# Layer 0 of a two-layer transformer block: feeding it from a transposed x, in eight granules of shift and scale

## The chip, the core and the metric

The kernel runs on one core of a Trainium2 chip. A core has a matrix engine (PE, TensorE), VectorE (DVE), ScalarE (ACT), GpSimd (POOL) and SyncE (SP), which here only issues DMAs. Each engine takes its instructions in program order; they meet through semaphores. DMAs issued from SP, ACT or POOL run on 16 DMA engines that the core's queues share. On-chip memory has 128 partitions; PE writes to eight PSUM banks of 128 x 512 float32. The metric is device time of the whole launch in microseconds.

## What is computed

The input x has 256 tokens of 2048 features; a second input c conditions both layers. Layer 0 mixes with differential attention, layer 1 with a state-space scan (SSD), and each layer ends in a SwiGLU feed-forward part. All in float32.

```python
c_act = silu(c)
for i in range(2):
    ada = c_act @ ada_w[i] + ada_b[i]                  # 2048 x 12288
    shift1, scale1, gate1, shift2, scale2, gate2 = split(ada, 6)
    h = rms_norm(x, norm1_g[i]) * (1 + scale1) + shift1
    m = diff_attention(h, ...) if i == 0 else mamba2_ssd(h, ...)
    x = x + gate1 * m
    h = rms_norm(x, norm2_g[i]) * (1 + scale2) + shift2
    x = x + gate2 * ((silu(h @ w_gate) * (h @ w_up)) @ w_down)
```

`diff_attention` projects h with `da_w_in` (2048 x 6144) to q, k and v of 16 heads; q and k are normalized per 64 features and rotated (a quarter of the features), two softmaxes per head are subtracted, and the result is normalized and projected with `da_w_out`.

## The kernel before

Nearly all time goes into streaming weights. A *unit* is 256 rows by 512 columns of a weight matrix, 512 KB, laid out on the host so that one DMA brings it into a `raw` buffer (7 of them, `rawp`). `split_unit` (line 244) issues the DMA on SP, lets ACT round it to a high part `wh` and, one unit later through the list `lagging`, lets DVE form the low part `wl = raw - wh`; there are four buffers of each. h is split in the same way into `ah` and `al`. `products` (276) then multiplies a unit with one block of 128 tokens in six matmuls of 512 columns (high x high, high x low, low x high for two groups of 128 features), so a unit costs twelve for both blocks.

The order of instructions is written out by a small planner while the program is built. `fifo` holds what is still to be written: weight units (`u`, at most four), units used raw (`a`, at most four) and plain calls (`c`). `push_unit` (260) and `push_raw` (267) write the DMA and casts at once and queue the matmuls; `pop` (224) writes the oldest. Each written weight unit is a `tick` (193): it lets one step of every generator in `active` be written (epilogues and attention heads are generators that yield between dependent steps), starts a new attention part from `pending` every four steps (`PACE`), and may write *jobs*. A job is one unit of 128 rows by 1024 columns of `ada_w` for one of the later shift, scale and gate vectors: a DMA and one DVE multiply-add into `acc` (`ada_job`, 426). `room` (185) holds jobs back when the charges booked for DVE or DMA are more than `METER` = 10,000 ns ahead of those for PE. A finished gate half is summed over the partitions by two POOL all-reduces (`fin_gate`, 508); a finished shift or scale half is summed by PE into columns (`to_cols`, 460).

**The start of layer 0.** The conditioning c comes in as 16 rows and is transposed by PE with an identity that POOL makes first; so are three tables of columns (norm gains and biases, class `Columns`, 361). `push_mods` (763) computes shift1 and scale1 for a quarter, 512 features, each from eight raw units: for each group of 128 rows PE multiplies c, repeated 32 times, with the unit in one of four 32-column strips; then ACT copies the bank, and `finish` sums and turns it into columns with four small matmuls. x is loaded as two blocks of tokens between the first units; ACT squares and scales it, PE transposes each quarter (32 transposes of 128 x 128 in all), and `Norm.finish` (546) applies scale and shift on DVE and splits h. `item` (1071) sets what happens before each raw unit: from the second quarter on it interleaves, per quarter, eight weight units of the first four (`N_EARLY`) projections, with the sixteen raw units of the next. `push_early` (1004) adds each such projection up over the quarters: two units share two PSUM banks, then ACT copies (first quarter) or DVE adds the banks to `part`.

After the last quarter the four early projections are completed (`complete`, 855: for q and k the generator `epilogue`, 807, with POOL's reciprocal root of the norms and rotary products `rt`), and the other eight of the twelve projections run over all 2048 rows in eight units each. `complete` of a q or k of head group 2 or 3 must first let all three parts of attention of the group two before have begun; if they haven't, it writes steps until they have. Attention (`attend`, 892) uses POOL for the norm of a head group's output (`oss`, `orr`). The output projection follows; before its last group's units `flush_steps` (216) writes all steps that are left. Jobs run in the order shift2, scale2, gate1; what is left of them is written by `flush_jobs` in the output projection.

`cols0.st` and the tiles for c and for the normalized x are taken from buffers that attention uses later (`raw`, pool `dp`).

Of the kernel before, what the change touches and what calls it, by code (L numbers as in the profile page):

```python
# [33 lines left out]
N_EARLY = 4  # L34
EPI = 3
ADA_UNITS = 140
# [51 lines left out]
def block_kernel(ctx: ExitStack, tc: tile.TileContext, x, c, positions, norm1_g, norm2_g, ada_w, ada_b,  # L88
                 ffn_gu, ffn_dn, da_in, da_out, q_g, k_g, lq1, lk1, lq2, lk2, subln_g,
                 ssd_in, conv_w, conv_b, dt_bias, a_log, d_skip, ssd_ng, ssd_out, out, upto="all"):  # L90
    nc = tc.nc
    ada_quarters = Units(ada_w, D, 256, chunks_of(2 * D))
    ada_rows, o = [], ada_quarters.end
# [173 lines left out]
    def push_raw(w, row, col, fn):  # L267
# [93 lines left out]
    class Columns:  # L361


        def __init__(self, groups):

            self.groups = groups
            self.st = rawp.tile([128, 8, 128], F32, tag="raw", name="stage")
            for i, (_, aps) in enumerate(groups):
                r = 0
                for a in aps:  # L370
                    pool.dma_start(self.st[r:r + a.shape[0], i, :], a)
                    r += a.shape[0]

        def finish(self, i):
            t = self.groups[i][0]
            n = t.shape[1]
            ps = bank("wk")
            pe.transpose(ps[:, :n], self.st[:n, i, :], ident[:n, :n])
            dve.tensor_copy(t, ps[:, :n])

    gcols = const.tile([128, 65], F32, name="gcols")
    bias_cols = [const.tile([128, 64], F32, name=f"bias{l}") for l in range(2)]
    bias_rows = ada_b.rearrange("l (v k p) -> l v k p", v=6, p=128)
    crows = rowp.tile([16, 128], F32, tag="acc", name="crows", bufs=2)
    sp.dma_start(crows, c.rearrange("o (k p) -> (o k) p", p=128))
    cols0 = Columns([
                     (gcols, [norm1_g.rearrange("l (k p) -> (l k) p", p=128),
                              norm2_g.rearrange("l (k p) -> (l k) p", p=128), subln_g]),
                     (bias_cols[0], [bias_rows[0, v:v + 2].rearrange("v k p -> (v k) p") for v in (0, 3)]),
                     (bias_cols[1], [bias_rows[1, v:v + 2].rearrange("v k p -> (v k) p") for v in (0, 3)])])  # L390
    ps = bank("wk")
    pe.transpose(ps[:, :16], crows, ident[:16, :16])
    cT = const.tile([128, 16], F32, name="cT")
    act.activation(cT, ps[:, :16], AF.Silu)
# [276 lines left out]
    pha = ExitStack()  # L671
    dp = pha.enter_context(tc.tile_pool(name="dp", bufs=1))
    cT32 = dp.tile([128, 512], F32, tag="on", name="cT32", bufs=1).rearrange("p (k m) -> p k m", m=32)
# [11 lines left out]
    lv = cols0.st[:, 4:6, :].rearrange("p a (i d) -> p (a i) d", d=64)  # L685
# [77 lines left out]
    def push_mods(q, item):  # L763

        sl = slice(4 * q, 4 * q + 4)
        for vec in range(2):
            st = {}

            def use(raw, u, st=st, vec=vec):
                if u == 0:  # L770
                    st["ps"] = bank(("po", "wk")[vec])
                for a in range(2):
                    k = 2 * u + a
                    g = k % 4
                    pe.matmul(st["ps"][32 * g:32 * g + 32, :], cT32[:, k, :], raw[:, a, :], start=(k < 4),
                              stop=(k >= 12), tile_position=(0, 32 * g), skip_group_check=True)
                if u == 7:
                    st["sb"] = tmp("adasb")
                    act.copy(st["sb"], st["ps"])

            def finish(st=st, vec=vec):
                ps2 = bank("wk")
                for i in range(4):
                    pe.matmul(ps2[:, i:i + 1], st["sb"][:, i * 128:(i + 1) * 128], c32, start=True, stop=True)
                t = S0 if vec else T0
                dve.tensor_tensor(t[:, sl], ps2[:, :4], b_cols[0, vec][:, sl], op=ALU.add)
                if vec:
                    dve.scalar_tensor_tensor(t[:, sl], t[:, sl], 1.0, n1c[0][:, sl], op0=ALU.add, op1=ALU.mult)
            for u in range(8):
                item(8 * vec + u)  # L790
                push_raw(ada_quarters, u * 256, vec * D + q * 512, lambda raw, u=u, use=use: use(raw, u))
                if u == 2 and vec == 1:
                    call(shift_finish)
                if u == 5 and vec == 1:
                    call(lambda: [norm_a.transposes(b, q, xns[b, q]) for b in range(2)])
            if vec == 0:
                shift_finish = finish
        return finish

# [7 lines left out]
    def epilogue(nm, dst, n, src):  # L807
# [22 lines left out]
        for b in range(2):  # L830
            rt = dp.tile([128, 8, 16], F32, tag="rt", name="rt", bufs=2)
# [23 lines left out]
    def complete(n, src, in_psum):  # L855
# [6 lines left out]
        if in_psum:  # L862
            while ahead():
                step_all()
            if i < 2:
                tiles = []
                for b in range(2):
                    t = dp.tile([128, 512], F32, tag="qn", name="qn", bufs=2)
                    act.copy(t, src[b])
                    tiles.append(t)  # L870
                src = tiles

        def steps(src=src):
            while ahead():
                yield
            if i == 2:
                v = dp.tile([128, 2, 512], F32, tag="v", name="v", bufs=2)
# [3 lines left out]
            else:  # L881
                dst = dp.tile([128, 4, 256], F32, tag=f"{nm}T", name=f"{nm}T", bufs=2)
# [9 lines left out]
    def attend(hg, qb, heads):  # L892
# [22 lines left out]
        for cc in range(2):  # L915
            m, n = mx[:, 4 * cc:4 * cc + nh], sums[:, 4 * cc:4 * cc + nh]
            dve.tensor_reduce(m, s3[cc], axis=AX.X, op=ALU.max, negate=True)
            ex = dp.tile([128, 512], F32, tag=f"e{cc}", name=f"e{cc}", bufs=(3, 1)[cc])
# [52 lines left out]
        on = dp.tile([128, 512], F32, tag="on", name="on", bufs=1)  # L971
# [32 lines left out]
    def push_early(n, q, half):  # L1004
        hg, i = keys[n]
        if half == 0:
            part[n, "bk"] = Banks()
        bk = part[n, "bk"]

        def run(u):  # L1010
            for b in range(2):
                products(bk()[b], norm_a.h[q][b], half, u, 512, half == 0, half == 1)
        push_unit(wi, q * 512 + half * 256, i * D + hg * 512, 512, run)
        if half == 1:
            def collect():
                if q == 0:
                    tg = ("oh", "ol")[n % 2]
                    part[n] = [op_.tile([128, 4, 128], F32, tag=tg, name=f"part{tg}")
                               .rearrange("p a n -> p (a n)") for b in range(2)]
                for b in range(2):  # L1020
# [50 lines left out]
    def item(i, q):  # L1071
# [8 lines left out]
        if p == 3:  # L1080
            flush()
# [598 lines left out]
```

## Time and profile before

| | us |
|---|---|
| median of 3 runs | 2696.89 (2692.03 to 2699.83) |
| the profiled execution | 2695.24 |
| its span (first to last instruction) | 2692.9 |
| PE busy | 2644.4 (98%) |
| DVE, ACT, POOL busy | 1912.2, 1346.4, 253.8 |
| HBM read | 678.43 MB |

A line of an instruction listing gives start, duration, engine, line of the program, operation, output and inputs by tile name, shape and count; in brackets stands how long the engine was idle before it, and what ended that. Matmul durations overlap: two matmuls of 512 columns start 0.23 us apart while each shows 0.39. `PEclk` is the clock that PE was granted (1.00 is full). A line of a group gives the count, the busy time and the mean of one in ns. Line 115 is the helper through which all PE and DVE instructions pass; they are told apart by their tiles.

### The profile page before, as it was taken

How to read it: one execution, taken by the hardware profiler on the slowest of the kernel's cores; microseconds unless marked ns; L12 is line 12 of the kernel's file. 1: busy time of each engine (PE TensorE's matmuls, PEld its weight loads, DVE VectorE, ACT ScalarE, POOL GpSimd, SP SyncE). 2: the span in 40 equal slices, each digit the busy share in tenths (PEclk: the TensorE clock that was granted, in tenths of full speed). 3: DMA queues.
4: the chain of work that ended last, by engine and by line, in shares of the span. 5: the costliest groups of instructions: out<-in, count | busy, mean ns of one | idle time of the engine just before them, and what ended most of it. 6: DMA issues, size and time to landing. Idle time of an engine off the chain costs nothing.

```text
span 2692.9 us, 35740 instructions
## 1 busy us (share of the span) xinstructions
PE 2644.4 (98%) x13205; PEld 2188.2 (81%) x13205; DVE 1912.2 (71%) x2154; ACT 1346.4 (50%) x1996; POOL 253.8 (9%) x242
## 2 busy tenths in 40 slices
PE   6999998999999999999999999999999999999999
PEld 2577886888888888888999989988888888888887
DVE  2579897888888886777777787786654444446776
ACT  3356774554444444445646556665554444444443
POOL 1032331102111110001000010000000000000001
PEclk8999999999999999999999999999999999999999
DMA  8989997788999997785567576666746555556885
GB/s 316 323 279 313 332 313 270 246 298 319 341 352 332 333 334 248 276 289 201 165 218 241 198 250 215 224 219 199 224 153 190 188 191 190 189 188 230 282 289 182
DMA packets 192558, 682.98 MB, mean 254 GB/s; under 512 B 22128, under 2 KB 30624, under 8 KB 191104
## 3 DMA queue, kind: packets, MB, share of 16 engines
q1 hardware_dynamic: 190256, 678.59, 72.9%
q0 software_dynamic: 1696, 2.03, 0.3%
q8 instruction: 103, 1.69, 0.2%
q14 instruction: 71, 0.58, 0.1%
q10 hardware_dynamic: 432, 0.10, 0.0%
HBM read 678.43 MB, written 2.20 MB: 253 GB/s over the span
## 4 chain that ended last, share of the span: by engine, by line
PE 92%; DVE 3%; DMA 2%; ACT 1%; issue 1%; POOL 0%; SPq 0%; ACTq 0%; DVEq 0%
PE mm L115 73%; PE wk L115 15%; PE po L115 4%; DMA raw<-in_da_w_in 1%; DMA raw<-in_ada_w 1%; DVE wl L115 1%; DVE acc L115 1%; ACT wh L250 0%; DVE hm L115 0%; DVE res L115 0%; DVE x L115 0%; DVE partol L115 0%; ACT hm L560 0%; DMA raw<-in_da_w_out 0%; ACT ah L566 0%
## 5 line engine op out<-in xcount | busy, mean ns | idle before, releaser
L250 ACT CAST wh<-raw 128x1024 fp32r<-128x1024 f32 (+1 forms) x888 | 925.8, 1046 | 1143.5 <-PE mm L115 756.8
L115 DVE TENSOR_TENSOR wl<-raw,wh 128x1024 fp32r<-128x1024 f32 (+1 forms) x888 | 1117.8, 1266 | 533.4 <-ACT wh L250 532.1
L115 PE MATMUL mm<-wh,ah 128*128 128x512 f32 (+1 forms) x2560 | 1016.5, 397 | 5.7 <-ACT ah L566 2.9
L115 PE MATMUL mm<-wl,ah 128*128 128x512 f32 (+1 forms) x2560 | 999.8, 391 | 0.6 <-DVE wl L115 0.6
L115 PE MATMUL mm<-wh,al 128*128 128x512 f32 (+1 forms) x2560 | 999.6, 390 | 0.0
L115 PEld LDWEIGHTS mm<-wh,ah 128*128 128x128 f32 x2560 | 482.3, 188 | 125.2 <-issue 16.7
L115 PEld LDWEIGHTS mm<-wh,al 128*128 128x128 f32 x2560 | 482.2, 188 | 102.9 <-DVE al L115 1.5
L115 PEld LDWEIGHTS mm<-wl,ah 128*128 128x128 f32 x2560 | 482.6, 189 | 97.9 <-DVE wl L115 2.0
L115 DVE SCALAR_TENSOR_TENSOR acc<-raw,cT,acc 128x1024 f32<-128x1024 f32 x300 | 386.0, 1287 | 0.5
L514 POOL PARTITION_ALL_REDUCE gate<-acc x16 | 54.7, 3460 | 969.7 <-DVE acc L115 954.8
L115 PE MATMUL wk<-wl,ah 128*128 128x512 f32 x360 | 140.2, 389 | 0.0
L115 PE MATMUL wk<-wh,ah 128*128 128x512 f32 x360 | 140.2, 389 | 0.0
L115 PE MATMUL wk<-wh,al 128*128 128x512 f32 x360 | 140.1, 389 | 0.0
L115 PE MATMUL mm<-ah,wh 128*128 128x256 f32 x720 | 118.8, 284 | 0.0
L115 PE MATMUL mm<-al,wh 128*128 128x256 f32 x720 | 117.7, 283 | 0.0
L115 PE MATMUL mm<-ah,wl 128*128 128x256 f32 x720 | 117.7, 283 | 0.0
L115 PEld LDWEIGHTS mm<-ah,wh 128*128 128x128 f32 x720 | 100.2, 192 | 0.1
L115 PEld LDWEIGHTS mm<-ah,wl 128*128 128x128 f32 x720 | 100.2, 192 | 0.0
L115 PEld LDWEIGHTS mm<-al,wh 128*128 128x128 f32 x720 | 100.2, 192 | 0.0
L466 POOL PARTITION_ALL_REDUCE row<-acc x16 | 54.9, 3478 | 382.7 <-DVE acc L115 382.7
L115 PEld LDWEIGHTS wk<-wl,ah 128*128 128x128 f32 x360 | 67.6, 188 | 14.4 <-DVE wl L115 0.4
L115 PEld LDWEIGHTS wk<-wh,ah 128*128 128x128 f32 x360 | 67.6, 188 | 14.2
(307 smaller groups left out, 2020.6 us busy)
## 6 DMA issues: line engine op xcount, KB each, us to landing
raw<-in_ada_w SPq DMA_DIRECT2D x384, 512.0 KB, 5.0
raw<-in_ffn_w_gate_up SPq DMA_DIRECT2D x352, 512.0 KB, 4.3
raw<-in_ffn_w_down SPq DMA_DIRECT2D x176, 512.0 KB, 4.8
raw<-in_ssd_w_in SPq DMA_DIRECT2D x136, 512.0 KB, 4.5
raw<-in_da_w_in SPq DMA_DIRECT2D x96, 512.0 KB, 5.3
raw<-in_ssd_w_out SPq DMA_DIRECT2D x64, 512.0 KB, 4.4
raw<-in_da_w_out SPq DMA_DIRECT2D x32, 512.0 KB, 5.3
raw<-in_ssd_w_in SPq DMA_DIRECT2D x24, 384.0 KB, 4.9
```

What stands on the lines that cost most here:

```text
L115: return fn(dst, *a, **k)
L250: act.copy(wh[:, :, :n], raw[:, :, :n])
L466: pool.partition_all_reduce(row[:, o], acc[:, o], 128, ReduceOp.add)
L514: pool.partition_all_reduce(mods["G", key][:, o:o + 512], acc[:, i * 512:(i + 1) * 512], 128, ReduceOp.add)
```

## The change

Five things change.

- **Tables.** The host lays c, the norm gains and the biases of layer 0's and 1's shifts and scales out as one array of 128 x 209, brought in by one DMA on SP; the SSD columns are three DMAs on ACT's queue. `Columns` and its six transposes go.
- **x.** The host adds a transposed copy `x_t` of x, four pieces of 512 KB with features on the partitions; they are loaded first. `token_sums` squares them on ACT and adds on DVE, PE sums over the partitions, POOL forms the reciprocal root, and `scale_tokens` has PE spread it over all partitions and DVE multiply the transposed x with it. No transposes of x remain. x itself is loaded into the same tiles later, while the eighth projection is queued.
- **Granules.** Shift and scale come in eight granules of 256 features; the host interleaves 256 columns of each in one unit of 512 columns, so that a granule is eight raw units, one bank and one `finish`. The raw units have a ring of nine buffers of their own (`A_BUFS`) in a pool `first`, which is closed before pool `dp` opens. `norm_pair` applies scale and shift on ACT for two groups of 128 features and splits h.
- **Partial sums.** Six projections instead of four are added up early, over eight granules instead of four quarters: each unit has two banks of its own, and its two blocks are copied (first granule) or added by DVE. The six units of a granule are interleaved with the eight raw units of the next.
- **Jobs.** Gate1 comes before shift2 and scale2; jobs may start from the fifth granule on instead of from the second quarter.

```diff
-N_EARLY = 4
+N_EARLY = 6
+A_BUFS = 9
...
-        raw = rawp.tile([128, 2, 512], F32, tag="raw", name="raw")
+        raw = ring.tile([128, 2, 512], F32, tag="araw", name="araw", bufs=A_BUFS)
...
+    cols = const.tile([128, 209], F32, name="cols")
+    sp.dma_start(cols, columns_in)
...
-    def push_mods(q, item):
...
+    def push_mods(g, item):
+        st = {}
+        sl = slice(2 * g, 2 * g + 2)
+        def use(raw, u):
+            if u == 0:
+                st["ps"] = bank(("po", "wk")[g % 2])
...
+        def finish():
+            ps2 = bank("wk")
+            for i in range(4):
+                pe.matmul(ps2[:, i:i + 1], st["sb"][:, i * 128:(i + 1) * 128], c32, start=True, stop=True)
+            dve.tensor_tensor(T0[:, sl], ps2[:, 0:2], b_cols[0, 0][:, sl], op=ALU.add)
+            dve.tensor_tensor(S0[:, sl], ps2[:, 2:4], b_cols[0, 1][:, sl], op=ALU.add)
+            dve.scalar_tensor_tensor(S0[:, sl], S0[:, sl], 1.0, n1c[0][:, sl], op0=ALU.add, op1=ALU.mult)
+        for u in range(8):
+            item(u)
+            push_raw(ada_first, u * 256, g * 512, lambda raw, u=u: use(raw, u), first)
...
+    def token_sums():
+        held["sums"] = [tmp("xsum") for _ in range(2)]
+        for q in range(4):
+            sq = rawp.tile([128, 2, 512], F32, tag="raw", name="xsq").rearrange("p a n -> p (a n)")
+            act.activation(sq, x_quarter(q), AF.Square)
+            dve.tensor_reduce(held["sums"][q // 2][:, (q % 2) * 256:(q % 2 + 1) * 256],
+                              sq.rearrange("p (k t) -> p t k", k=4), axis=AX.X, op=ALU.add)
...
+    def scale_tokens():
+        ps = bank("wk")
+        for b in range(2):
+            o = slice(b * 128, b * 128 + 128)
+            pe.matmul(ps[:, o], held["r"][:, o], ident, start=True, stop=True)
+        for q in range(4):
+            v = x_quarter(q).rearrange("p (k t) -> p k t", k=4)
+            dve.tensor_tensor(v, v, ps[:, None, 0:256].to_broadcast([128, 4, 256]), op=ALU.mult)
+    def norm_pair(g):
...
+        hm = tmp("hm").rearrange("p (k t) -> p k t", k=2)
+        for i in range(2):
+            k = 2 * g + i
+            act.activation(hm[:, i, :], x_feature(k), AF.Identity, bias=T0[:, k:k + 1], scale=S0[:, k:k + 1])
+        act.copy(h[:, o, :], hm)
+        dve.tensor_tensor(l[:, o, :], hm, h[:, o, :].bitcast(F32), op=ALU.subtract)
...
-    def push_early(n, q, half):
...
+    def push_early(n, g):
...
+                products(bk()[b], norm_a.h[q][b], half, u, 512, True, True)
+        push_unit(wi, g * 256, i * D + hg * 512, 512, run)
+        def collect():
...
+                if g == 0:
+                    act.copy(part[n][b], bk()[b])
+                else:
+                    dve.tensor_tensor(part[n][b], part[n][b], bk()[b], op=ALU.add)
...
+    ada_job(0, 2, fin_gate("m0"), gate=True)
     ada_job(0, 3, fin_shift("f0", b_cols[0, 3]))
     ada_job(0, 4, fin_scale("f0", b_cols[0, 4], n2c[0]))
-    ada_job(0, 2, fin_gate("m0"), gate=True)
...
+    for q in range(4):
+        sp.dma_start(x_quarter(q), x_t[q])
...
+    def item(i, g):
+        if g == 0:
+            if i in (2, 4):
+                call(token_rstd if i == 2 else scale_tokens)
             return
+        at["p"] += 1
+        if i == 1:
+            call(finishes[g - 1])
+        elif i == 2:
+            call(lambda: normed(g - 1))
+        elif i == 3:
+            while g - 1 not in done:
+                pop()
+            todo.extend((n, g - 1) for n in range(n_early))
+            span.update({"from": at["p"], "to": at["p"] + 8, "n": len(todo)})
+        while todo and len(todo) * (span["to"] - span["from"]) > span["n"] * (span["to"] - at["p"]):
+            push_early(*todo.popleft())
...
+    def load_x():
+        for b in range(2):
+            sp.dma_start(xt[b], x[0, b * 128:(b + 1) * 128, :])
     for n in range(n_early, 12):
+        if n == n_early + 1:
+            call(load_x)
```

More of the change, by code (lines that the diff above doesn't have):

```diff
@@ L1098, in block_kernel @@
+    for k in range(max(3, len(todo))):
+        if k == 1:
+            call(finishes[7])
+        elif k == 2:
+            call(lambda: norm_pair(7))
+            call(open_dp)
         if todo:
```

253 lines of the change are left out of this document (92 added, 161 removed).

## The prediction

> **What bounds the kernel now.** I read the engine totals first, then busy time by stage, then the instructions in order of time at the two places where the matrix engine (PE) stands still.
>
> ```profile
> span 2692.9 us, 35740 instructions
> PE 2644.4 (98%) x13205; PEld 2188.2 (81%) x13205; DVE 1912.2 (71%) x2154; ACT 1346.4 (50%) x1996; POOL 253.8 (9%) x242
> ```
> ```profile
> core 0: us, PE busy (x) PEld busy (x) DVE busy (x) ACT busy (x) POOL busy (x), PEclk, DMA share, GB/s
> 0.00:50.00 50.00, 28.64 (x116) 9.14 (x117) 7.37 (x24) 15.21 (x33) 12.73 (x33) 0.87 0.91 323
> 50.00:165.00 115.00, 110.79 (x529) 65.85 (x528) 59.36 (x136) 39.86 (x53) 0.00 (x0) 0.97 0.90 320
> 200.00:440.00 240.00, 236.83 (x1231) 191.13 (x1229) 216.34 (x280) 164.77 (x434) 73.50 (x80) 0.99 0.90 317
> 440.00:480.00 40.00, 29.29 (x125) 23.15 (x124) 31.55 (x27) 14.67 (x26) 8.97 (x7) 0.87 0.73 249
> ```
>
> PE is the bound. It is idle 48.5 us in all, 21.4 of them before 50 us and 10.7 between 440 and 480 us; only these two places have much to give. From 200 to 440 us VectorE (DVE) is 90% busy and the DMA share is 0.90, so little more fits there. Why PE waits at the start:
>
> ```profile
> 39.33 1.35 SPq L247 DMA_DIRECT2D raw<-in_da_w_in  x1
> 40.75 0.16 DVE L115 TENSOR_TENSOR S<-wk,bias 128x4 f32<-128x4 f32 x1 [7.76 <-PE wk L115]
> 46.35 1.04 ACT L250 CAST wh<-raw 128x1024 fp32r<-128x1024 f32 x1 [1.22 <-DMA raw<-in_da_w_in]
> 47.45 0.67 PE L115 MATMUL mm<-wh,ah 128*128 128x512 f32 x1 [2.67 <-ACT wh L250]
> ```
>
> The first projection matmul runs at 47.45 us, behind 16 shift and scale units, x, four more units and its own weights. And around 450 us:
>
> ```profile
> 436.61 0.20 POOL L978 TENSOR_TENSOR orr<-orr,r 128x4 f32<-128x4 f32 x1
> 444.72 7.12 POOL L514 PARTITION_ALL_REDUCE gate<-acc  x2 [7.91 <-DVE wl L115]
> 459.82 0.19 POOL L975 TENSOR_TENSOR oss<-oss,r 128x4 f32<-128x4 f32 x1 [7.98 <-issue]
> 461.81 0.20 POOL L978 TENSOR_TENSOR orr<-orr,r 128x4 f32<-128x4 f32 x1
> ```
> ```profile
> 462.50 1.36 PE L115 MATMUL wk<-ident,on 128*128 128x128 f32 x4 [9.08 <-ACT on L983]
> 463.51 0.78 PE L115 MATMUL mm<-wh,oh 128*128 128x512 f32 x1
> 464.08 0.63 PE L115 MATMUL mm<-wl,oh 128*128 128x512 f32 x1
> 464.51 0.63 PE L115 MATMUL mm<-wh,ol 128*128 128x512 f32 x1
> ```
> ```profile
> L514 POOLq MODIFY_POOL_CONFIG  x10: 6/11/16, 437.0 to 1960.9; - x10
> ```
>
> The gate's two all-reduces sit between the last attention heads' POOL steps. POOL changes its configuration at 437.0 us, starts the reduces 7.9 us after its last step, and does nothing for another 7.98 us behind them: it is closed for 436.8 to 459.8, 23 us. The last head's scaling waits for that, and PE idles 9.08 us.
>
> **The change, part by part.** E stands for one weight unit of a partial projection (12 matmuls of 512 columns), A for one shift/scale unit.
>
> *Earlier start.* Before the first E, 25 units of 0.524 MB had to come in (16 A, four units' worth of x, 4 A, 1 E: 13.1 MB); now 17 (4, 8, 4, 1: 8.9 MB) and 0.1 MB of columns. At 323 GB/s of the first 50 us that is 28 us; with the cast of 1.04 us the first matmul comes at 29. The same sum for before gives 42 where 47.45 was measured, because six free buffers were handed round; A now has nine of its own and the weights keep seven. I take 30 (29 to 35). The new way to h isn't later: x is in by 10 us; four squares and four strided reduces take 1.2 to 1.4 us each (twice the durations for 512 columns below); POOL issues its small loads first, 9 us in the rows below, of which seven stage loads go, so the reciprocal root is there before 20 us; four multiplies of 1024 columns at 1.2 to 1.3 us end before 26, and the first scale needs the ninth A, some 22 us.
>
> ```profile
> L421 ACT ACTIVATE junk<-x 128x512 f32<-128x512 f32 x8 | 4.9, 618 | 0.0
> L115 DVE TENSOR_REDUCE qss<-sq 128x8 f32<-128x512 f32 x8 | 5.1, 679 | 0.4 <-ACT sq L814 0.4
> 13.89 0.76 POOL L677 DMA_DIRECT2D posi<-in_positions  x1
> 22.21 0.54 POOL L687 DMA_DIRECT2D stage<-in_da_lambda_k  x1
> ```
>
> *Eight granules of 6 E and 8 A.* What they cost PE:
>
> ```profile
> 92.16 0.50 PE L115 MATMUL mm<-wh,ah 128*128 128x512 f32 x1
> ...
> 95.14 1.05 PE L115 MATMUL po<-raw,cT 128*32 128x512 f32 x4
> 96.12 0.50 PE L115 MATMUL mm<-wh,ah 128*128 128x512 f32 x1
> ```
> ```profile
> 103.02 1.07 PE L115 MATMUL wk<-raw,cT 128*32 128x512 f32 x8
> 104.02 1.05 PE L115 MATMUL wk<-c,adasb 128*128 128x1 f32 x8
> 104.93 0.48 PE L115 MATMUL mm<-wh,ah 128*128 128x512 f32 x1
> ```
>
> An E is 2.98 us (92.16 to 95.14). A lone A is 0.98, and two neighbouring A together 1.00: they fill different column groups. The transfer to columns is 0.91. Before, a quarter held 8 E, 16 A mostly in pairs, two column transfers and eight transposes: about 35 us of PE work, yet quarters are 40.5 us apart in the rows below, 12.6 MB at 311 GB/s. There DMA was the limit. Now the interleave of 6 and 8 leaves two pairs and four lone A, so a granule is 6 x 2.98 + 6 x 0.98 + 0.91 = 24.7 us, while its 14 units need 7.3 MB, 23 us at 320. PE becomes the limit. Each E now ends in two DVE additions from PSUM:
>
> ```profile
> L115 DVE TENSOR_TENSOR partoh<-partoh,mm 128x512 f32<-128x512 f32 x12 | 7.9, 683 | 2.4 <-PE mm L115 2.4
> L115 DVE TENSOR_TENSOR wl<-raw,wh 128x1024 fp32r<-128x1024 f32 x45 | 55.5, 1233 | 48.6 <-ACT wh L250 48.4
> 123.73 0.16 DVE L115 TENSOR_TENSOR S<-wk,bias 128x4 f32<-128x4 f32 x1 [1.87 <-PE wk L115]
> 164.24 0.16 DVE L115 TENSOR_TENSOR S<-wk,bias 128x4 f32<-128x4 f32 x1
> 165.85 0.50 PE L115 MATMUL mm<-wh,ah 128*128 128x512 f32 x1 [1.65 <-ACT ah L566]
> ```
>
> That is 84 additions of 0.68 us instead of 24, 41 us more. In a granule DVE has 6 x 1.23 + 12 x 0.68 and about 1.2 for the norm, 17 of 25 us, so they lie beside PE. Once in a granule the program drains its list before the new h is taken; then the next low part is queued behind the last addition, 1.37 + 1.23 against one A of 0.98: up to 1.6 us in which PE waits. I take 1.0 and a period of 25.6 (24.7 to 26.3). The first interval has only four E and starts cold: from 30 the second column transfer ends near 49. Six periods more put the last at 203, with 40 of 96 E done. Before it was at 164.2 with 24 done; 16 E more at 12 x 0.228 us are 43.8, and 1.65 of waiting behind it go: 209.7. **Start: -7 us** (-14 to +4).
>
> *Gate first.* The wait of 9.08 us at 453 us goes, and with it the slow matmuls behind it (0.43 to 0.57 us apart above, 0.23 normally), about 1.5. What is late next is the same head's own chain, hardly longer than the matmuls at hand. **-10 us** (-11 to -4).
>
> What is moved comes down elsewhere. By the planner's own charges (E: 2616 PE, 1460 DMA, 1130 DVE; a job 1460 and 1130; at most 10,000 ahead) the first gate half is complete about 50 E after the first, the second about 65; the first four q and k epilogues start between 43 and 55. POOL's closure of 23 us then falls among their steps. Behind it wait the rotary products on POOL, DVE's additions to them one step later, every low part behind these, and so PE; four weight buffers and one to three steps cover some 11 to 17 us. It can also miss:
>
> ```profile
> 263.16 0.79 POOL L975 TENSOR_TENSOR oss<-oss,r 128x4 f32<-128x4 f32 x1 [24.26 <-ACT osq L970]
> ```
>
> POOL has such gaps of 24 us. I take **+4** for both halves (0 to +30). The Trainium skill, "GPSIMD Engine Reference", section 2.1 "Instruction dispatch", says that the first call of a freshly loaded kernel costs about 6 us of code loading that shows as no instruction; by that figure the closure would be 19 us and the slower case below 2703 instead of 2711. This trace has 7.9 before and 7.98 behind, so the rows stand. DVE suffers too:
>
> ```profile
> 492.37 6.49 POOL L514 PARTITION_ALL_REDUCE gate<-acc  x2 [30.36 <-DVE acc L115]
> 492.59 7.49 DVE L115 TENSOR_TENSOR wl<-raw,wh 128x1024 fp32r<-128x1024 f32 x3 [0.36 <-ACT wh L250]
> ```
>
> Three low parts took 7.49 instead of 3.7 us during the reduces: 4 us per half, now in a stage where DVE is 90% busy; it is in the upper bound.
>
> *Six projections early.* Their epilogues start within six E, and the seventh projection is complete eight E later. It must not overwrite q before all three parts of head group 0 have begun, and these begin four steps apart; so the program steps about six times with no matmul between. **+2** (0 to +12).
>
> *x again, columns, order of jobs.* 2.1 MB of x are loaded again in a stage with a tenth of DMA free, 24 us of 240 against 6.6: hidden, **+1** with DVE's denser jobs (0 to +8). The transposes of h are counted in the period; those of the column tables, here and in layer 1, are six of 0.25 us: **-0.5**.
>
> Sum: -7 - 10 + 4 + 2 + 1 - 0.5 = -10.5. The profiled execution took 2695.2 us (its span and 2.3 us around it), so 2684.7; it lay 1.7 below the median of the runs shown, so the forecast is **2686**.
>
> **The rivals.** *Both gains whole:* the closures meet gaps, the steps are covered, no drain stall: -14 - 11 + 1, about 2673. For it: the 24 us gap; against it: epilogues crowd where the reduces fall. *The granules eat the start:* a stall of 2 us or more per granule and lone A throughout; start +2, the rest as forecast, 2695. The change then would not do what it says. For it: the period counts seven times; against: DVE has 8 us free per granule. *Slower:* POOL's closures in the middle of attention. If each half holds PE 15 us (23 less 8 for three weight units), that is +30 - 17 + 1, about 2711. It turns the sign once the two together exceed 17 us. For it: the 9 us seen after a single closure, with epilogues much denser at the new place; against: at the tail no weights were left to multiply, here there are.
>
> **How the numbers follow.** Forecast 0.46 (own range 2677 to 2695), gains whole 0.20, start eaten 0.14, slower 0.20. Faster by over 0.3%, 8 us, about what a measurement can tell: 0.70 of the first and all of the second, 0.52. Same: 0.14 and 0.14, 0.28. Slower 0.20. The range, 2667 to 2712, leaves a tenth at each end.
>
> **What would show it.** Right: first projection matmul near 30 us; column transfers 25 to 26 us apart with PE dense; the partial sums finished near 215 us; no PE wait of 9 us around 450 us; the all-reduces inside attention. Wrong: granules nearer 28 us, a PE wait of over 8 us behind the all-reduces, or DVE ending the waits between 200 and 420 us. If DMA ends most waits in the granules, the rate I assumed is wrong.

## The result, and the profile after

The changed kernel takes 2720.08 us (median of 4 runs, 2715.38 to 2721.11) against 2694.68 us for the kernel before: ratio 1.0087, 95% interval 1.0071 to 1.0103. It is slower, and the time lies 8 us above the upper end of the range. The profiled execution took 2715.38 us.

Span and engine totals of the changed kernel, then its busy time by stretch with the stretches of the prediction, and one stretch more:

```profile
span 2713.7 us, 35705 instructions
```
```profile
0.00:50.00 50.00, 34.31 (x151) 17.58 (x152) 21.43 (x33) 18.78 (x25) 8.63 (x24) 1.00 0.96 354
50.00:165.00 115.00, 112.97 (x512) 68.09 (x512) 85.68 (x155) 43.56 (x56) 0.00 (x0) 1.00 0.91 346
200.00:440.00 240.00, 203.56 (x1001) 162.42 (x1001) 199.76 (x265) 155.56 (x420) 93.36 (x98) 0.93 0.75 264
440.00:480.00 40.00, 36.91 (x205) 28.38 (x204) 33.02 (x47) 23.27 (x71) 6.11 (x7) 1.00 0.77 264
...
200.00:350.00 150.00, 113.56 (x536) 88.17 (x536) 115.89 (x158) 91.64 (x259) 64.26 (x67) 0.90 0.66 228
```

The last stretch in the kernel before:

```profile
200.00:350.00 150.00, 147.37 (x769) 119.79 (x768) 137.12 (x178) 103.59 (x270) 46.34 (x49) 0.98 0.90 316
```

The columns are length, then busy time of PE, PE's weight loads, DVE, ACT and POOL, the granted clock, DMA share and GB/s. Both ends improved: PE is idle 15.7 us before 50 us (21.4 before) and 3.1 between 440 and 480 (10.7 before). But between 200 and 350 us PE is now idle 36.4 us, where it was idle 2.6, and the granted clock there fell from 0.98 to 0.90. DVE, ACT and the DMA are less busy there too: they wait for one another. Only POOL is busier, 64.3 us instead of 46.3, because the reduces now fall there. By stages PE's idle time changed by -8.3 us (0 to 200), +33.8 (200 to 350) and -7.7 (400 to 550). That makes 17.8 of the span's 20.8; the rest is PE's busy time, 2647.3 us instead of 2644.4.

POOL's instructions in the changed kernel, around the two gate halves:

```profile
238.44 1.31 POOL L855 TENSOR_TENSOR rt<-partol,Bk 128x64 f32<-128x64 f32 x1
247.30 6.49 POOL L487 PARTITION_ALL_REDUCE gate<-acc  x2 [7.55 <-issue]
260.95 0.31 POOL L853 TENSOR_TENSOR rt<-partol,Bq 128x64 f32<-128x64 f32 x1 [7.16 <-issue]
...
319.25 0.31 POOL L999 TENSOR_TENSOR orr<-orr,r 128x4 f32<-128x4 f32 x1
327.71 6.49 POOL L487 PARTITION_ALL_REDUCE gate<-acc  x2 [8.16 <-DVE acc L116]
341.15 0.19 POOL L386 TENSOR_SCALAR qr<-qss 128x8 f32<-128x8 f32 x1 [6.95 <-DVE acc L116]
```

From 239.75 to 260.95 us POOL does nothing for the attention: 7.55 us before the reduces, 6.49 for both, 7.16 behind them. The change of configuration stands in POOL's queue on both sides, under the line of the reduces from 239.9 us on and under that of `rt` at 253.7:

```profile
L487 POOLq MODIFY_POOL_CONFIG  x10: 5/8/11, 239.9 to 1981.8; - x10
L853 POOLq MODIFY_POOL_CONFIG  x2: 87/88/88, 253.7 to 253.8; - x2
```

Such a time in which POOL is closed to attention is called a *closure* below. The second one, 319.56 to 341.15, is alike. Who waits behind the first, on DVE and then on PE:

```profile
242.94 0.75 DVE L116 TENSOR_SCALAR acc<-raw,cT 128x1024 f32<-128x1024 f32 x1
...
261.57 0.40 DVE L116 TENSOR_TENSOR partol<-partol,Aq 128x128 f32<-128x128 f32 x1 [17.89 <-POOL rt L855]
```
```profile
246.55 0.39 PE L116 MATMUL mm<-wh,al 128*128 128x512 f32 x1
262.44 1.08 PE L116 MATMUL wk<-ident,partol 128*128 128x128 f32 x4 [15.50 <-DVE partol L116]
```

This is the queue that the prediction named: the rotary product `rt` on POOL is late, DVE's next instruction in order needs it, every low part stands behind that, and PE runs dry. POOL stops at 239.75 and PE's last matmul ends at 246.94: the work in hand covered 7 us.

### The profile page after: what moved, and what is told of

It is laid out like the page before. It is cut to its first block, busy times and chain, and to the rows that moved or that the text cites. A ratio compares the mean times of both kernels' runs of the same rounds, so it can differ in the third digit from the quotient of the medians.

```text
span 2713.7 us, 35705 instructions
## 1 busy us (share of the span) xinstructions
PE 2647.3 (98%) x13186; PEld 2186.9 (81%) x13186; DVE 1945.6 (72%) x2188; ACT 1348.3 (50%) x1986; POOL 242.9 (9%) x229
## 4 chain that ended last, share of the span: by engine, by line
PE 90%; DVE 4%; issue 2%; ACT 2%; DMA 1%; POOL 1%; SPq 0%; DVEq 0%; ACTq 0%; POOLq 0%
PE mm L116 71%; PE wk L116 14%; PE po L116 4%; DVE acc L116 1%; DVE wl L116 1%; DMA raw<-in_da_w_in 1%; ACT wh L251 0%; DVE mx L116 0%; ACT e L942 0%; DMA araw<-in_ada_w 0%; DVE xsum L116 0%; POOL gate L487 0%; DMA raw<-in_ssd_w_in 0%; ACT hm L533 0%; DVE qss L116 0%
## 5 line engine op out<-in xcount | busy, mean ns | idle before, releaser
L116 PEld LDWEIGHTS wk<-wh,al 128*128 128x128 f32 x360 | 67.6, 188 | 14.0
```

The source lines that it names most:

```text
L116: return fn(dst, *a, **k)
```

## Experiments

Each kernel was measured in a set with the kernel before on the same chip, which had medians of 2691.8 to 2694.7 us. The table gives each kernel's median less that of the kernel before in its own set, in us; differences between kernels are taken from these. "First" and "last" say whether the gate's jobs run ahead of those of shift2 and scale2 or behind them.

| gate's sums | kernel before | change, 4 early | change, 6 early |
|---|---|---|---|
| POOL, last | 0 | -6.7 | +8.6 |
| POOL, first | +12.7 | -1.1 | +25.4 (the change) |
| PE, first | -4.9 | -12.6, -14.2 | -2.3 |
| PE, last | | -8.1 | |

PE's idle time by stage, length less PE's busy time in the windows:

| kernel | 0 to 50 | 50 to 200 | 200 to 350 | 400 to 550 |
|---|---|---|---|---|
| before | 21.4 | 5.2 | 2.6 | 12.1 |
| the change | 15.7 | 2.5 | 36.4 | 4.4 |
| gate last on POOL, 6 early | 16.2 | 2.6 | 11.7 | 17.1 |
| gate last on POOL, 4 early | 15.3 | 6.4 | 2.1 | 17.0 |
| gate first on PE, 6 early | 16.2 | 2.5 | 13.6 | 2.9 |
| the same and two short all-reduces | 17.1 | 2.5 | 26.1 | 2.8 |
| gate first on PE, 4 early | 16.3 | 6.3 | 8.5 | 2.3 |
| gate first on PE, 6 early, pairs | 17.1 | 0.5 | 12.9 | 2.8 |

**1. The gate last again.**

```diff
-    ada_job(0, 2, fin_gate("m0"), gate=True)
     ada_job(0, 3, fin_shift("f0", b_cols[0, 3]))
     ada_job(0, 4, fin_scale("f0", b_cols[0, 4], n2c[0]))
+    ada_job(0, 2, fin_gate("m0"), gate=True)
```

> Changed kernel with the gate jobs back behind shift and scale; all else of the change stays. Theory C (POOL's configuration change closes it for about 21 us twice in the middle of attention, and PE loses about 30 us there): the closures leave the middle, the tail's wait of about 9 us returns, so about 2700 us (2694 to 2706), and between 200 and 350 us PE idles about 10 us instead of 36. Rival B (six early projections crowd the epilogues and DVE): PE still idles 25 us or more there, and the time is 2712 or more, up to 2730. Third (granules, start): no change to the middle, 2715 or more.

2700.92 us, ratio 1.0028 (1.0019 to 1.0037). In the windows and among PE's instructions:

```profile
200.00:350.00 150.00, 138.27 (x728) 110.86 (x729) 138.80 (x199) 112.05 (x312) 57.03 (x68) 0.99 0.82 285
```
```profile
464.25 1.35 PE L116 MATMUL wk<-ident,on 128*128 128x128 f32 x4 [8.76 <-ACT on L1004]
```

The wait at the tail is back (8.76 us), the idle time of the middle falls from 36.4 to 11.7. Moving the gate alone made the change 17 us slower (25.4 less 8.6). But 8.6 us above the kernel before remain, although the gate stands where it stood: something else of the change costs.

**2. The gate first, its sums on PE.** A matrix of ones on PE adds up the partitions; four such sums of 512 columns are eight instructions, 4.3 us of PE in the groups of this run.

```diff
+    def sum_on_pe(row, acc, hf):
+        for i in range(2):
+            yield from take("wk")
+            ps = bank("wk")
+            pe.matmul(ps, ones.to_broadcast([128, 128]), acc[:, i * 512:(i + 1) * 512], start=True, stop=True)
+            yield
+            o = hf * 1024 + i * 512
+            act.copy(row[:, o:o + 512], ps)
+            give("wk")
...
+            if key == "m0":
+                active.append(sum_on_pe(mods["G", key], acc, hf))
+                return
```

> Changed kernel, gate jobs still first, but the m0 gate's four sums over the partitions are made by PE with a matrix of ones (512 columns each, one bank, copied out by ScalarE) instead of POOL's all-reduces; about 4 us of PE work more. Theory C: no closure in the middle and none at the tail: about 2688 us (2682 to 2695). Rival B: still 2710 or more. If C is right, this run and the one with the gate last differ by the tail, about 10 us.

2689.97 us, ratio 0.9986 (0.9976 to 0.9995). That is 28 us less than the change (25.4 and 2.3). Estimated with the 4.3 us that the sums cost PE, the two closures cost about 32. Theory C holds for them. Still, start and tail had promised more than 2.3 us below the kernel before: PE idles 13.6 us in the middle. Its waits there:

```profile
215.21 0.50 PE L116 MATMUL mm<-wh,ah 128*128 128x512 f32 x1 [0.51 <-DVE partoh L116]
220.02 0.47 PE L116 MATMUL mm<-wh,ah 128*128 128x512 f32 x1 [1.75 <-DVE partol L116]
224.73 0.47 PE L116 MATMUL mm<-wh,ah 128*128 128x512 f32 x1 [1.73 <-DVE partoh L116]
232.42 0.47 PE L116 MATMUL mm<-wh,ah 128*128 128x512 f32 x1 [1.99 <-DVE partoh L116]
```

And DVE in the same kernel, between two of them:

```profile
218.06 1.21 DVE L116 TENSOR_TENSOR wl<-raw,wh 128x1024 fp32r<-128x1024 f32 x1
219.19 1.27 DVE L116 TENSOR_TENSOR partol<-partol,mm 128x512 f32<-128x512 f32 x2
220.39 1.27 DVE L116 SCALAR_TENSOR_TENSOR acc<-raw,cT,acc 128x1024 f32<-128x1024 f32 x1
221.58 1.27 DVE L116 TENSOR_REDUCE qss<-sq 128x8 f32<-128x512 f32 x2
222.77 1.22 DVE L116 TENSOR_TENSOR wl<-raw,wh 128x1024 fp32r<-128x1024 f32 x1
```

This is the last granule. From low part to low part DVE has 4.7 us of work without a gap, and PE's units start 4.7 us apart (220.02 to 224.73): each waits until DVE has added two banks to the partial sums `partol` or `partoh` and they are free again. In the granules before nothing of the epilogues was there yet.

**3. Four early projections, the gate first on POOL.**

```diff
-N_EARLY = 6
+N_EARLY = 4
```

> Changed kernel with four early projections instead of six; gate units still first. Theory C: the closures stay amid the epilogues of attention, so no gain of that kind: 2708 to 2725 us. The granules hold only 4 units of the weights against 8 of shift and scale, so the start may also lose some us. Rival B: the crowding goes, 2690 to 2698.

2691.23 us, ratio 0.9995 (0.9984 to 1.0007): both missed in part. The closures still cost, with one long wait behind the second:

```profile
304.23 1.09 PE L116 MATMUL wk<-ident,qn 128*128 128x128 f32 x4 [13.90 <-DVE qn L116]
```

But the time is 26.5 us below the change's (25.4 and 1.1), as low as the rival had it. The two causes don't simply add.

**4. The kernel before, only with the gate first.**

> Kernel before with the gate jobs ahead of shift and scale, nothing else. Theory C: the tail gains 10, the middle loses 20 to 35 us, so slower than before: 2705 to 2720 us. Rival B: the tail's gain alone, about 2685 us.

2705.03 us, ratio 1.0042 (1.0028 to 1.0056): slower, with none of the other changes. Two waits of PE among its instructions are behind the closures:

```profile
252.92 1.35 PE L115 MATMUL wk<-ident,on 128*128 128x128 f32 x4 [6.13 <-ACT on L983]
...
312.82 1.35 PE L115 MATMUL wk<-ident,on 128*128 128x128 f32 x4 [4.83 <-ACT on L983]
```

**5, 6, 7. Four early with the gate on PE; the kernel before with the gate first on PE; four early with the gate last.** They fill the first table. Their edits are those of 1 to 3 together.

> Changed kernel with four early projections and the m0 gate's sums on PE. Theory (closures and the early projections' crowding on DVE are two separate costs, and start and tail gain 8 and 10 us as forecast): the run with four early projections and POOL's all-reduces idled PE 19.7 us between 200 and 350 us; without closures 3 to 6, so 2669 to 2679 us. Rival (with four early projections the closures cost nothing, its 2691 us comes from something else): 2685 or more.

> Kernel before, gate jobs first, their sums on PE; nothing else of the change. Theory: the tail's 10 us are gained, and nothing is lost in the middle: 2680 to 2687 us. With POOL's all-reduces the same order took 2705 us. Rival (it is the jobs' order, not the closures, that costs the middle): 2700 or more.

> Changed kernel with four early projections and the gate last: the start alone. Theory: the start gains some 8 us and nothing else moves: 2681 to 2688 us; six early projections with the gate last took 2701, so the two added ones cost 13 to 20 us. Rival (the granules eat the start, or three us of waits per added projection are not the matter): 2692 or more.

2680.45 (ratio 0.9958, 0.9943 to 0.9973), 2688.11 (0.9983, 0.9973 to 0.9992) and 2686.35 (0.9979, 0.9970 to 0.9989). The fifth kernel, measured again in five rounds, had 2678.97:

> The kernel with four early projections and the gate's sums on PE once more, in five rounds, as the version that beats both: 2680 us, ratio 0.994 to 0.997 of the kernel before.

The kernel with PE's sums and four early was 1.5 us slower than expected at the first measurement and inside the range at the second. The kernel before with PE's sums gained 5 us, not 10: its idle time from 400 to 550 us falls by 7.6, and PE gives 4.3 back for the sums. Moved ahead on POOL (row two against row three of the table), the closures cost 11.5 to 13 us with four early, 18 in the kernel before and 28 with six, and 4.3 more each for what PE's sums take: two closures each time, three prices. So it isn't the closures alone that set the price. What they meet there is the likely reason, but no run varies that by itself. The start alone (four early, gate last) gains 6.7 us.

**8 and 10. Pausing the jobs.** The jobs' multiply-add is 1.27 of DVE's 4.7 us per unit. A job is written when the credit `acc`, which grows by `rate` with each unit, has reached one. In run 8 the rate is zero while the last granule is issued; jobs already credited still ran, six between 208 and 233 us, so the edit didn't do what it was for. Run 10 clears the credit too.

```diff
-    call(lambda: ada.update(rate=1.5))
+    call(lambda: ada.update(rate=0.0, acc=0.0))
     for n in range(n_early):
         push_early(n, 7)
+    call(lambda: ada.update(rate=1.5))
```

> Changed kernel, six early projections, gate sums on PE, but no shift, scale and gate jobs are started while the last granule's six units are issued; the same jobs run later. Theory (between 205 and 236 us DVE has 5 us of work for each unit: low part 1.22, two additions 1.28, a job 1.28, squares' sums 1.27, against 2.98 of PE): without the 1.28 the PE waits of 1.7 to 2.0 us behind the partial sums fall to 0.5 to 0.8, PE idles 3 to 5 us less there, 2684 to 2688 us against 2690. Rival (the burst of steps or ScalarE sets the pace there): the waits stay, 2689 or more.

> Changed kernel, six early projections, gate sums on PE; the jobs' credit is set to zero as well as their rate while the last granule is issued, so that jobs really pause there (the run before still had six jobs between 208 and 233 us). Read between 205 and 236 us alone: theory (DVE sets the pace of the last granule): at most two jobs are left there and the PE waits behind the partial sums fall from 1.75 to under 1 us; rival (steps or ScalarE): they stay. The whole time may rise for what the later jobs meet behind it, 2690 to 2702 us.

2698.86 and 2698.41 us, 5.8 and 4.4 above the kernel before, where the same kernel without the pause lies 2.3 below it. PE's waits in run 10:

```profile
219.59 0.47 PE L116 MATMUL mm<-wh,ah 128*128 128x512 f32 x1 [1.79 <-DVE partol L116]
223.37 0.47 PE L116 MATMUL mm<-wh,ah 128*128 128x512 f32 x1 [0.80 <-DVE partoh L116]
231.07 0.47 PE L116 MATMUL mm<-wh,ah 128*128 128x512 f32 x1 [2.02 <-DVE partoh L116]
```

Only the second wait shrinks, by 0.93 us. Three jobs were left between 208 and 217 us, one more than expected, so the first wait had its job still; the third had none and stayed. That the jobs set the pace there is refuted but for this one wait. Ahead of the third, DVE itself now stands still for ACT's squares `sq`, where without the pause it had waited 0.56 us for them:

```profile
227.91 1.28 DVE L116 TENSOR_REDUCE qss<-sq 128x8 f32<-128x512 f32 x2 [1.76 <-ACT sq L848]
```

There the epilogue's work on ACT sets the pace once the job is gone; the shares of the other pieces on DVE and ACT were not separated. And jobs put off cost more later than they gave: nothing is gained by shifting them.

**11. Four early, the gate last, on PE.**

> Changed kernel with four early projections, gate last, its sums on PE: no POOL closure, the jobs' order as before. With POOL's reduces last it took 2686, with PE's sums first 2680. Theory (at the tail it is the closure that costs, not the place of the gate): the wait of 8.9 us near 450 us falls below 4 and the time is 2677 to 2682 us. Rival (a gate finished last holds up the residual whoever sums it): 2685 or more.

2685.85 us, ratio 0.9976 (0.9965 to 0.9987): the rival. It is no faster than POOL's reduces in the same place. PE's waits:

```profile
446.44 1.21 PE L116 MATMUL wk<-ident,on 128*128 128x128 f32 x4 [2.15 <-ACT on L1017]
...
495.38 0.80 PE L116 MATMUL wk<-wh,oh 128*128 128x512 f32 x1 [5.03 <-ACT gate L488]
```

The wait at the last head shrinks from 8.91 to 2.15 us, but now PE waits 5.03 for a copy of the gate row. A gate that is finished last is late whoever sums it; the tail's gain needs both, POOL open and the gate early.

**12. PE's sums, and a short all-reduce beside them.** It separates the change of configuration from the reduces' own time.

```diff
                 active.append(sum_on_pe(mods["G", key], acc, hf))
+                pool.partition_all_reduce(small(8, "idle"), acc[:, 0:8], 128, ReduceOp.add)
```

> Changed kernel, six early projections, gate sums on PE, and beside them one all-reduce of 8 columns on POOL for each half, whose result is not used. Without it 2690 us, with the four all-reduces of 512 columns 2720. Theory (it is the change of configuration, some 8 us on each side, that closes POOL, not the reduces' own 13 us): 2705 to 2716 us, and POOL shows gaps of 7 us or more on both sides of a short reduce. Rival (the reduces' own time and DVE's slowing by it): 2690 to 2696.

2709.72 us, ratio 1.0060 (1.0043 to 1.0076): 18 us more than without it (15.8 and 2.3). Both kernels make the sums on PE, so these 18 are to be set against the 32 us of the closures with four full reduces: over half. POOL around the first:

```profile
240.02 1.30 POOL L869 TENSOR_TENSOR rt<-partol,Bk 128x64 f32<-128x64 f32 x1
248.68 0.43 POOL L497 PARTITION_ALL_REDUCE idle<-acc  x1 [7.37 <-issue]
256.14 0.31 POOL L867 TENSOR_TENSOR rt<-partol,Bq 128x64 f32<-128x64 f32 x1 [7.04 <-issue]
```

A reduce of 0.43 us closes POOL for 14.8, and the second one, of 1.43 us, for 19.4 (7.63 ahead of it and 10.29 behind). So over half of the price is the change there and back; the other 14 us come with the summing, which makes the closures longer and slows DVE.

**9, 13, 14, 15. Why six early projections cost 10 us where POOL stays open.** Five early; five with three q and k epilogues instead of four, by the order q0, k0, v0, v1, q1, k1; six with room for four epilogues at once; four with two epilogues. All have the gate first on PE.

```diff
-    keys = [(0, 0), (0, 1), (0, 2), (1, 0), (1, 1), (1, 2),
+    keys = [(0, 0), (0, 1), (0, 2), (1, 2), (1, 0), (1, 1),
```
```diff
-EPI = 3
+EPI = 4
```

> Changed kernel with five early projections and the gate sums on PE. With four it took 2680, with six 2690. Theory (each early projection more adds units in which DVE has 4 to 5 us of work for 2.98 of PE, and epilogues that come at once): 2683 to 2687 us, between the two. Rival (the sixth alone costs, because the seventh projection then has to wait for attention): 2679 to 2682, as with four.

> Changed kernel, gate sums on PE, five early projections, but the order of projections is q0, k0, v0, v1, q1, k1: the five hold three epilogues of q and k instead of four (v has none). Theory (it is the fourth epilogue, crowded into the last granule, that costs): 2678 to 2683 us, as four early projections did with three epilogues. Rival (the number of early projections and their additions): 2687 to 2691, as the other five did.

> Changed kernel, gate sums on PE, six early projections, with room for four epilogues at once instead of three. Theory (ScalarE and DVE are crowded by the epilogues themselves): no gain, 2688 to 2695 us. Rival (the fourth epilogue waits for a place and holds up attention): 2680 to 2685.

> Changed kernel, gate sums on PE, four early projections in the order q0, k0, v0, v1: two epilogues instead of three. Theory of the epilogues: 2674 to 2680 us. Rival (only the limit of three at once counts): 2680 as with three; if the first attention of head group 1 now comes too late, 2683 or more.

Five took 2689.22 us (ratio 0.9981, 0.9971 to 0.9990), 4.8 below the kernel before; six lies 2.3 below it, and the intervals overlap. Five is thus about as slow as six, and both expectations missed. Five with three epilogues took 2689.97 (0.9992, 0.9983 to 1.0001): the epilogues' number isn't it. Six with room for four took 2695.72 (1.0007, 0.9997 to 1.0016): no gain, as the crowding theory had it, rather a loss. Four with two epilogues took 2672.91 (0.9929, 0.9916 to 0.9941), the fastest of all, 6 to 8 us below four with three, as the theory of the epilogues had it, which five with three epilogues doesn't bear out. Its idle time from 200 to 350 us is 4.5 us instead of 8.5, at a granted clock of 1.00 in every 50 us from 200 to 450.

What five and six share, and four has not, stood in another view: the groups by tile, here the matmuls of shift and scale at the start (count, busy time, mean in ns). The change first, then four early with PE's sums:

```profile
L116 PE MATMUL po<-araw,cT 128*32 128x512 f32 x128 | 27.1, 698 | 10.6 <-DMA araw<-in_ada_w 10.6
...
L116 PE MATMUL wk<-araw,cT 128*32 128x512 f32 x128 | 26.0, 604 | 0.2 <-DMA araw<-in_ada_w 0.2
```
```profile
L116 PE MATMUL po<-araw,cT 128*32 128x512 f32 x128 | 23.6, 666 | 11.1 <-DMA araw<-in_ada_w 11.1
L116 PE MATMUL wk<-araw,cT 128*32 128x512 f32 x128 | 21.7, 605 | 1.2 <-DMA araw<-in_ada_w 1.2
```

The same 256 matmuls are busy for 53.1 us against 45.3 (53.2 with five early). Among six or five weight units the units of shift and scale mostly run alone, 0.98 us each; among four they run in pairs, 1.00 for two.

**17 and 18. Six early, but the units of shift and scale kept in pairs;** in 18 also the order with v1 ahead.

```diff
-        while todo and len(todo) * (span["to"] - span["from"]) > span["n"] * (span["to"] - at["p"]):
+        while i % 2 == 0 and todo and len(todo) * (span["to"] - span["from"]) > span["n"] * (span["to"] - at["p"]):
```

> Changed kernel, gate sums on PE, six early projections; weight units of a granule are issued only ahead of every second shift or scale unit, so that these stay in pairs. Theory (six early projections cost 8 of their 10 us because lone shift and scale units take 0.98 us and pairs 1.00): their busy time falls from 53.3 to about 46 us and the time from 2690 to 2680 to 2684 us. Rival (the crowding of additions and epilogues from 205 us on costs it all): their busy time falls and the time stays at 2688 or more, since PE then only waits longer behind DVE.

> The same with the order of projections q0, k0, v0, v1, q1, k1, which won 6 to 8 us where four were early. Theory (there one epilogue fewer crowded the start of attention; six hold the same four either way): no more than 3 us from the kernel with pairs alone, 2678 to 2684. Rival (the order itself helps attention): 2673 to 2677.

2682.42 us (0.9961, 0.9948 to 0.9975) and 2683.54 (0.9967, 0.9954 to 0.9979). The same groups in run 17:

```profile
L116 PE MATMUL po<-araw,cT 128*32 128x512 f32 x128 | 23.2, 672 | 11.3 <-DMA araw<-in_ada_w 11.3
L116 PE MATMUL wk<-araw,cT 128*32 128x512 f32 x128 | 22.1, 605 | 0.6 <-DMA araw<-in_ada_w 0.6
```

45.3 us, and 7 us off the time (-9.4 against -2.3): of the 10 to 12 us between four and six early, some 7 are lone shift and scale units. The middle stays at 12.9 us of idle PE (13.6 without the pairs). The order with v1 ahead gives nothing where six are early; why it gives 6 to 8 us where four are, stays open.

## Why the prediction was wrong

**The step that failed** is "I take **+4** for both halves (0 to +30)". The closures cost about 32 us (28 between the change and run 2, and 4.3 of PE's sums), at or above the upper end. The mechanism and the queue behind it were named, and stood as the rival "POOL's closures in the middle of attention" with 2711 us; the forecast took the lower end because POOL has gaps of 24 us and because weights in hand "cover some 11 to 17 us". They covered 7: DVE's next instruction waited for `rt` since 243.7 us, the low parts of the units already loaded stood behind it, and a weight without its low part can't be multiplied. So the first closure of 21.2 us left 15.5 us of PE standing still, at the rival's own figure of 15 a half; the second was spread over waits of 2 to 4 us and a slower clock (0.89 from 300 to 350 us), and its longest wait follows DVE, not POOL's queue (shown below). The gap of 24 us that spoke for a miss lay between 238.9 and 263.2 us in the kernel before, the very time of the first closure; but in the change POOL had rotary products on either side of it.

The rival's sum, +30 - 17 + 1, leaves out the forecast's +2 and -0.5; with them it gives 2712, and the sign turns at 14.5 us instead of 17.

**"Six projections early: +2 (0 to +12)"** was mis-sized as well. Run 1 against run 7, six early against four with the gate last, gives it directly: 15.3 us (8.6 and 6.7). PE's idle time between 200 and 350 us makes 9.6 of it (11.7 against 2.1). The shift and scale units that run alone make 7.0 (busy for 52.9 us against 45.9); the prediction had booked these under the start. Up to 200 us PE is idle 3.0 us less, which leaves 13.6 of the 15.3. PE's longer idle time behind 400 us, 17.1 against 12.1 in the kernel before, is no part of it: it stands with four early too (17.0). Behind the idle time of the middle is not the burst of steps with no matmul between, which was priced, but first of all the last granule: five waits for DVE's additions make 6.4 of run 1's 11.7 us, and the units start up to 4.8 us apart instead of 3.0, while DVE runs almost without a gap on low parts, additions, jobs and the first epilogues. Which of these sets the pace was not separated beyond the jobs and the one wait for ACT. The prediction had counted DVE's slack over a whole granule, 17 of 25 us, and not in the last one, which alone meets the epilogues.

With 32 and 15 in the places of +4 and +2, the sum would give about 2727 us, 7 more than was measured: the two terms don't simply add.

**The start, -7**, was about right. The first projection matmul starts at 31.91 us (30 forecast), the column transfers come 24.1 to 25.3 us apart and the last is finished at 200.05 (203 forecast), PE's idle time up to 200 us falls by 8.3, and the start alone gains 6.7 us, though with four early. The agreement is in part luck, because there the gain is made of something else: in run 7 PE's idle time as a whole is nearly the old one (47.6 us against 48.5; 4.9 less up to 200 us, 4.9 more between 400 and 550), and PE's busy time is 7.5 us less (2636.9 against 2644.4). Shift and scale alone account for more than that, since their matmuls were busy for 58.4 us in the kernel before, where run 7 has 45.9:

```profile
L115 PE MATMUL po<-raw,cT 128*32 128x512 f32 x128 | 30.7, 720 | 3.2 <-DMA raw<-in_ada_w 2.4 <-DVE cT L115 0.7
L115 PE MATMUL wk<-raw,cT 128*32 128x512 f32 x128 | 27.7, 661 | 4.9 <-DMA raw<-in_ada_w 4.9
```

The lone units' 0.98 us were in the prediction's sum. That they could be had for half by another interleave was not seen; run 17 shows 7 us for it. The reference point of 209.7 for the kernel before was early: counting twelve matmuls a unit, its 41st unit starts at 216.6, because head steps run in between. That doesn't change the term much, as those steps must be done later in the changed kernel. One of the signs failed: DVE's last addition to the partial sums ends at 234.7 us, where "near 215" was to show that the forecast was right. That figure didn't follow from the forecast's own sum either: 203 and eight units of 2.74 us are 225.

**The gate first, -10** held roughly: the wait of 9.08 us is gone, idle time from 400 to 550 us falls by 7.7, and run 6 gains 4.9 us while it spends 4.3 on PE's sums, about 9 together. **The reload of x and the tables** were too small to be seen beside the rest and weren't tried alone. **DVE under the reduces:** the second gate half shows

```profile
327.66 3.37 DVE L116 SCALAR_TENSOR_TENSOR acc<-raw,cT,acc 128x1024 f32<-128x1024 f32 x1
331.21 2.02 DVE L116 SCALAR_TENSOR_TENSOR mx<-sums,nlam,mx 128x2 f32<-128x2 f32 x1
333.26 0.88 DVE L116 SCALAR_TENSOR_TENSOR e<-e,mx,e 128x256 f32<-128x256 f32 x2
```
```profile
333.89 1.09 PE L116 MATMUL wk<-ident,e 128*128 128x128 f32 x4 [4.20 <-DVE e L116]
```

a multiply-add in 3.37 us instead of 1.28, slowed as the low parts were in the kernel before, and an operation on two columns in 2.02, both while the reduces ran (327.71 to 334.20 us). The attention weights `e` stand behind these on DVE, and PE waits 4.20 us for them: the longest wait of the second closure. Run 12, with almost no reduce time, costs 10 us less than the change although it also pays 4.3 for PE's sums. Part of these 14 us is DVE's slowing, part the longer closure; they weren't separated.

The Trainium skill, "GPSIMD Engine Reference", section 2.1 "Instruction dispatch", gives about 6 us for the first call of a freshly loaded kernel. In the change and at the first closure of run 12, 7.37 to 8.16 us lie ahead of the reduces and 6.95 to 7.16 behind them, so the measured rows stand, and the way back is paid as well.

**What beats both.** Four early projections in the order q0, k0, v0, v1, with the gate first and summed on PE, take 2672.91 us, ratio 0.9929 (0.9916 to 0.9941) to the kernel before.

## What to carry to other kernels

A short instruction that makes an engine change its configuration is priced by how long that engine is closed to everyone, and by what is queued in order behind the first one who waits; count the cover as work that can really be done then, not as buffers that are full. Work moved off the end of a stage isn't free at its new place just because the engine is lightly used there: the same two closures cost 16 to 32 us in three settings. And when an interleave is changed, look whether small instructions that ran side by side now stand alone.

## What was not expected of the hardware

A PARTITION_ALL_REDUCE of 0.43 us closes POOL for 14.8 us, 7.37 before it and 7.04 behind; with 6.49 us of reduces it is 21.2. After PE had stood still for 15.5 us its granted clock was 0.50 for 3.6 us, 0.82 for the next 4.0 and 1.00 from 270 to 280 us:

```profile
262.40:266.00 3.60, 3.56 (x22) 2.69 (x22) 3.56 (x6) 0.69 (x1) 0.15 (x1) 0.50 0.28 79
266.00:270.00 4.00, 4.00 (x19) 3.09 (x18) 3.96 (x5) 0.00 (x0) 3.75 (x4) 0.82 0.91 257
```

A multiply-add of 1024 columns on DVE took 3.37 us instead of 1.28 while a reduce ran on POOL.
